# A decoder layer on one core: x added to five row blocks by accumulating transfers, the residual kept in the output's place, and two kinds of endings

## The chip, the cores and the metric

One NeuronCore of a Trainium2 chip runs the whole kernel; the metric is the device time of one execution in microseconds. The engines are TensorE (PE, with its weight loads PEld), VectorE (DVE), ScalarE (ACT), GpSimd (POOL) and SyncE (SP, which only issues DMA transfers here). Each engine works its own instructions in the order in which the program wrote them, and waits on semaphores for the others.

## The reference

One layer of a hybrid decoder, 1024 rows of 1024 columns, float32:

```python
h = rms_norm(h_res, pre_mix_g)            # h_res = 16 meta rows, then x
proj = h @ w_in                           # q1 q2 k1 k2 v u
o = rms_norm(diff_attention(...), subln_g) * 0.8
y = rms_norm(glu(gelu(s5_ssm(u))), ssm_out_g)
mix = concat([o, y]) @ w_out
h_res = h_res + rms_norm(mix, post_mix_g)           # the first residual
h = rms_norm(h_res, pre_ffn_g)
f = (silu(h @ w_gate) * (h @ w_up)) @ w_down
h_res = h_res + rms_norm(f, post_ffn_g)             # the second residual
return h_res[:, 16:]
```

The meta rows are dropped from the output, so both residuals are needed for the 1024 rows of x alone.

## The kernel before, in words

Rows are handled in eight blocks of 128, numbered t_ = 0 to 7. The mixed output of block t_ collects in the SBUF tile `part[t_]` (128 x 1024): matmuls leave `mix` banks in PSUM, and DVE adds them to the tile. Attention ends with the late blocks first; the order in which the blocks are complete is `ORD` = 6, 7, 4, 5, 2, 3, 0, 1.

`chain_t` then makes the first residual of a block: ACT squares `part` with a sum (`jk<-part`), DVE and POOL make the root (`rstd`: a tiny DVE instruction, then a power on POOL), DVE scales the block by the root and the gain (`part<-part,ms,gpm`), and DVE or POOL, whichever the planner thinks is done earlier, adds x, which SP has loaded into a tile `xr` (a ring of three). The sum stands in `xr`. ACT squares it, ACT's queue stores it to the DRAM tensor `h_d` (`act_dma`), a second root is made, and ACT or DVE writes the scaled block back to `part`. `ht_stream` transposes that on PE; from there the FFN's products start.

The FFN is a recursion with seven products in place of eight, in float32 split into a high and a low part (`unit`: a cast on ACT, a difference on DVE or POOL). Weight units stand in slots of SBUF (`slot`), of which `sl_add` opens a number with each pool. The products of gate and up end in PSUM banks `PA` and `PS`; those of the down projection in `dn` banks, which `xacc_stream` adds to accumulators X (`XA`, `XS` in the profile). Between the two, the units of silu(gate) * up go to DRAM (`fu_d`) and come back as `dA` and `dS`.

`out_t` ends a block: SP loads the first residual from `h_d` into `hr`, DVE adds the last banks, ACT squares the two halves with sums (`jkf`), DVE or POOL multiplies each half by the gain `gpf`, DVE and POOL make the root (`ms<-ssf`, then the power), DVE multiplies each half by the root and adds the residual in one instruction (`XA<-XA,ms,rr` and the like), and SP stores the half to the output. Blocks 4 to 7 and 0 to 3 end in pairs, q = t_ % 4 going from 0 to 3; the last pair is blocks 7 and 3.

The order of all instructions is written by a planner when the program is built (`Plan`). Every stream above is a generator that yields the engine and the tiles it needs next; the planner keeps a clock for each engine from its own prices, and always lets the stream go on whose need is met earliest. So a new price or a new step changes the order of what follows. `TUNE` holds small offsets for streams by stretches of the planner's own time.

Of the kernel before, what the change touches and what calls it, by code (L numbers as in the profile page):

```python
# [8 lines left out]
F32 = mybir.dt.float32  # L9
# [29 lines left out]
SCRATCH = 1024  # L39
SEG = 40.0  # L40
# [337 lines left out]
def W(fn):  # L378
    return fn, "pe"
# [13 lines left out]
def build(tc, I, out):  # L393
# [12 lines left out]

    st = ExitStack()
# [72 lines left out]
    h_d = dr.tile([NX, D], F32, name="h_d")  # L480
# [1380 lines left out]
    def chain_stream():  # L1861
        yield W(lambda: "wo" in flag and "kv" in flag)
        om = open_pool(om_es, "om")
        gpm = om.tile([P, D], F32, name="gpm")
        sp.dma_start(out=gpm, in_=I["post_mix_g"][0].partition_broadcast(P))
        S["om"] = om, gpm, om.tile([P, D], BF16, name="jk")
        wp["early"] = {}
        for n, t_ in enumerate(ORD):
            yield W(lambda: n < NXR or ORD[n - NXR] in hdone)
            xr = T_(om, [P, D], F32, "xr", "xr", NXR)  # L1870
            sp.dma_start(out=xr, in_=I["x"][0, t_ * P:(t_ + 1) * P, :])
            xrs[t_] = xr
        yield W(lambda: len(hdone) == T and "raw0" in flag and "hT" in flag)
        om_es.close()
        pt_es.close()
        flag["om"] = True
        plan.fill = None

    def early_stream():
        yield W(lambda: "om" in S and len(xrs) >= XR0)  # L1880
# [13 lines left out]
    XR0 = 2  # L1894
    xrs, odone, hdone = {}, set(), set()

    def chain_t(t_):
        yield W(lambda: t_ in odone and t_ in xrs and wp.get("y", 0) > t_)
        om, gpm, jk = S["om"]
        xr, pt = xrs[t_], part[t_]  # L1900
# [10 lines left out]
        else:  # L1911
# [3 lines left out]
            eng = "pool" if plan.end("pool", 2.0) < plan.end("dve", 2.0) else "dve"  # L1915
            yield G(eng, pt, xr)
            (pool if eng == "pool" else dve).tensor_tensor(xr, pt, xr, ALU.add)
# [3 lines left out]
        act_dma(h_d[t_ * P:(t_ + 1) * P, :], xr)  # L1921
# [12 lines left out]
    def ffn_open():  # L1934
# [13 lines left out]
        sl_add(pa, 6)  # L1948
# [16 lines left out]
    CS = [2, 3, 3, 3]  # L1965
    DORD = ["A11", "S3", "S2", "S1", "A12", "S4", "A22"]
# [433 lines left out]
    def out_t(t_):  # L2400
        q = t_ % 4
        yield W(lambda: "dn" in flag)
        hr = raw_new()
        sp.dma_start(out=hr, in_=h_d[t_ * P:(t_ + 1) * P, :])
# [6 lines left out]
        for d, n in zip(ds, names):  # L2411
# [8 lines left out]
            e = less("dve", "pool")  # L2420
            yield G(e, xs[d])
            engs[e].tensor_tensor(xs[d], xs[d], gpf[:, d * 512:d * 512 + 512], ALU.mult)
# [6 lines left out]
        for d in ds:  # L2429
            cs = slice(d * 512, d * 512 + 512)  # L2430
            yield G("dve", ms, xs[d])
            dve.scalar_tensor_tensor(xs[d], xs[d], ms, hr[:, cs], ALU.mult, ALU.add)
            sp.dma_start(out=out[0, t_ * P:(t_ + 1) * P, cs], in_=xs[d])
        raw_free(hr)
# [53 lines left out]
```

## Time and profile before

| | us |
|---|---|
| median of 3 runs | 1256.05 |
| lowest and highest run | 1255.34, 1260.98 |
| the profiled execution, its own time | 1258.01 |
| its span, first to last instruction | 1256.2 |
| busy in the span: PE / PEld / DVE / ACT / POOL | 1193.3 / 1009.7 / 936.7 / 585.8 / 637.8 |

The span is what the rows below are taken from; times in them count from its start. A busy share over the whole span mixes stages with different limits.

### The profile page before, as it was taken

What the parts mean: (1) busy time and instruction counts of PE and PEld (TensorE: products, weight loads), DVE (VectorE), ACT (ScalarE), POOL (GpSimd) and SP (SyncE); (2) the same over time, 40 slices, a digit from 0 to 9 for tenths busy, and PEclk for the clock granted to TensorE, in tenths of its full rate; (3) what the DMA queues carried; (4) which work ended last, traced back from release to release, by engine and by line L of the source; (5) the groups of instructions that cost most, each with busy time, mean ns of one, the idle gap of its engine ahead of it and who ended that gap; (6) DMA issues with size and microseconds to landing.
All of it is one profiled execution on the core that took longest, in us unless ns stands there. A gap on an engine that the chain in (4) does not pass through costs nothing.

```text
span 1256.2 us, 19391 instructions
## 1 busy us (share of the span) xinstructions
PE 1193.3 (95%) x6808; PEld 1009.7 (80%) x6808; DVE 936.7 (75%) x1678; ACT 585.8 (47%) x1203; POOL 637.8 (51%) x663
## 2 busy tenths in 40 slices
PE   8999989999999999888999999999999989999994
PEld 6999979988888788667878888888888868888873
DVE  5978886664857879898667877668665876466998
ACT  6323323245756556656456456454555544222122
POOL 1015556413423023555666666677676765455735
PEclk9999989999999999989999999999999999999997
DMA  8254434316421013232244434344334479766563
GB/s 245 78 108 102 99 96 98 98 60 188 167 69 51 26 51 118 84 109 85 85 167 163 156 101 167 135 177 153 112 135 161 187 275 413 277 216 227 197 251 134
DMA packets 155490, 182.89 MB, mean 146 GB/s; under 512 B 72017, under 2 KB 122481, under 8 KB 155393
## 3 DMA queue, kind: packets, MB, share of 16 engines
q1 hardware_dynamic: 153056, 177.38, 42.4%
q10 hardware_dynamic: 2336, 4.26, 0.9%
q8 instruction: 54, 0.88, 0.3%
q14 instruction: 44, 0.35, 0.1%
HBM read 117.52 MB, written 61.44 MB: 142 GB/s over the span
## 4 chain that ended last, share of the span: by engine, by line
PE 73%; DVE 10%; POOL 6%; DMA 4%; issue 3%; ACT 2%; SPq 1%; DVEq 0%; POOLq 0%; ACTq 0%
PE PS L246 17%; PE PA L246 12%; PE dn L246 12%; PE pqk L246 6%; PE mix L246 6%; PE pv L246 5%; PE pu L246 3%; PE s L246 3%; DVE XS L246 2%; PE z L246 2%; DVE part L246 1%; DVE XA L246 1%; PE aT L246 1%; PE pm L246 1%; DMA x<-in_x 1%
## 5 line engine op out<-in xcount | busy, mean ns | idle before, releaser
L246 PE MATMUL PS<-BT,uS 128*128 128x512 f32 x792 | 193.8, 399 | 2.9 <-ACT uS L246 1.8
L246 PEld LDWEIGHTS PS<-BT,uS 128*128 128x128 f32 x792 | 149.9, 190 | 40.5 <-ACT uS L246 2.3
L246 PE MATMUL PA<-B,uA 128*128 128x512 f32 x528 | 134.3, 403 | 3.3 <-DVE B L246 3.1
L246 PE MATMUL dn<-dS,dS 128*128 128x512 f32 x528 | 126.3, 399 | 5.3 <-DMA dS<-fu_d 5.3
L246 PEld LDWEIGHTS dn<-dS,dS 128*128 128x128 f32 x528 | 101.0, 192 | 28.9 <-DMA dS<-fu_d 5.7
L246 PEld LDWEIGHTS PA<-B,uA 128*128 128x128 f32 x528 | 100.4, 191 | 28.0 <-DVE B L246 3.4
L246 PE MATMUL dn<-dA,dA 128*128 128x512 f32 x396 | 93.7, 393 | 2.4 <-DVE dA L246 2.4
L246 PEld LDWEIGHTS dn<-dA,dA 128*128 128x128 f32 x396 | 74.2, 188 | 19.8 <-DVE dA L246 2.8
L246 ACT CAST uS<-rr 128x512 fp32r<-128x512 f32 x84 | 50.4, 618 | 53.1 <-DVE rr L246 37.9
L246 PE MATMUL pqk<-wlo,hTh 128*128 128x256 f32 x256 | 73.0, 285 | 1.8 <-DVE wlo L246 1.8
L246 PE MATMUL pqk<-whi,hTh 128*128 128x256 f32 x256 | 74.4, 291 | 0.0
L246 PE MATMUL pqk<-whi,hTl 128*128 128x256 f32 x256 | 72.8, 284 | 0.0
L246 ACT ACTIVATE rr<-rr,gffT 128x256 f32<-128x256 f32 x168 | 72.2, 498 | 0.6 <-DMA rr<-in_w_up 0.6
L246 POOL TENSOR_TENSOR uS<-rr,uS 128x512 fp32r<-128x512 f32 x41 | 60.9, 1497 | 21.1 <-ACT uS L246 18.6
L246 POOL TENSOR_TENSOR uA<-rr,uA 128x512 fp32r<-128x512 f32 x30 | 43.5, 1451 | 53.2 <-ACT uA L246 47.4
L246 PE MATMUL PS<-B,uS 128*128 128x512 f32 x264 | 65.5, 397 | 0.0
L246 PE MATMUL PA<-BT,uA 128*128 128x512 f32 x264 | 65.4, 396 | 0.0
L246 POOL TENSOR_TENSOR ms<-ms,mhalf 128x1 f32<-128x1 f32 (+1 forms) x41 | 25.5, 625 | 70.8 <-DVE ms L246 58.4
L246 DVE TENSOR_TENSOR uA<-rr,uA 128x512 fp32r<-128x512 f32 x30 | 31.7, 1057 | 39.7 <-ACT uA L246 39.2
L246 DVE TENSOR_REDUCE nmx<-s 128x1 f32<-128x528 f32 (+8 forms) x60 | 47.9, 809 | 16.4 <-PE s L246 16.3
L246 PEld LDWEIGHTS PA<-BT,uA 128*128 128x128 f32 x264 | 49.7, 188 | 12.1
L246 PEld LDWEIGHTS PS<-B,uS 128*128 128x128 f32 x264 | 49.7, 188 | 12.1
(467 smaller groups left out, 3326.1 us busy)
## 6 DMA issues: line engine op xcount, KB each, us to landing
fu_d<-fS SPq DMA_DIRECT2D x44, 512.0 KB, 2.8
dS<-fu_d SPq DMA_DIRECT2D x44, 512.0 KB, 5.2
fu_d<-fA SPq DMA_DIRECT2D x33, 512.0 KB, 3.1
dA<-fu_d SPq DMA_DIRECT2D x33, 512.0 KB, 5.1
rr<-in_w_up SPq DMA_DIRECT2D x22, 512.0 KB, 4.4
rr<-in_w_gate SPq DMA_DIRECT2D x20, 512.0 KB, 4.8
rr<-in_w_down SPq DMA_DIRECT2D x10, 512.0 KB, 5.7
raw<-qk_d SPq DMA_DIRECT2D x6, 768.0 KB, 5.7
```

Of the source, the lines that this page charges most:

```text
L246: r = real(*a, **kw)
```

## The change

In the first residual, the first five blocks of `ORD` (`NXA = 5`: 6, 7, 4, 5, 2) no longer load x into `xr`. Their sum is made in `part` itself: POOL's queue issues a transfer from x in DRAM onto the tile that adds what it brings (`add_dma`, `accum_op`). The store of the sum follows directly in the program, on ACT's queue, ahead of the square; for the other three blocks the add and the store stay as they were. All eight blocks are stored to the output tensor's own rows instead of `h_d`, which is gone.

In the endings, only the blocks with q = 3 (`LATE`: 7 and 3) load the residual back, from the output, and end as before, with the multiplications by the gain put on DVE except for one half. The other six blocks multiply by root and gain in one DVE instruction, and POOL's queue issues a transfer for each half that adds it to the output in DRAM.

A pool of weight slots gets seven in place of six, and the early loads of weights wait for the same number of x loads as before, counted anew. The planner's prices for the new transfers are in `add_dma`.

```diff
--- before.py
+++ after.py
@@ -37,6 +37,7 @@
 
 BIAS = {}
 SCRATCH = 1024
+NXA = 5
 SEG = 40.0
 TUNE = {
     0: {'gate_stream': -0.04, 'ssm_u_stream': -0.23, 'proj_stream': 0.39, 'ynorm_stream': 0.0},
@@ -404,6 +405,13 @@
         plan.clk["act"] += 0.5
         plan.sent(out, src, plan.clk["act"])
 
+    def add_dma(out, src):
+
+        plan.flush((plan.tid(out), plan.tid(src)))
+        nc.gpsimd.dma_start(out=out, in_=src, accum_op=ALU.add)
+        plan.clk["pool"] = max(plan.clk["pool"], plan.wrote(src, "pool")) + 1.0
+        plan.sent(out, src, plan.clk["pool"] + 3.5)
+
     st = ExitStack()
     st.enter_context(tc.manual_schedule())
     cp = st.enter_context(tc.tile_pool(name="cp", bufs=1))
@@ -477,7 +485,6 @@
     u_d = dr.tile([L, 512], F32, name="u_d")
     v_d = dr.tile([L, 512], F32, name="v_d")
     qk_d = dr.tile([H, L, 384], F32, name="qk_d")
-    h_d = dr.tile([NX, D], F32, name="h_d")
     y_d = dr.tile([NX, 512], F32, name="y_d")
     fu_d = dr.tile([NF // 2, 7, P, D], F32, name="fu_d")
 
@@ -1865,8 +1872,10 @@
         sp.dma_start(out=gpm, in_=I["post_mix_g"][0].partition_broadcast(P))
         S["om"] = om, gpm, om.tile([P, D], BF16, name="jk")
         wp["early"] = {}
-        for n, t_ in enumerate(ORD):
-            yield W(lambda: n < NXR or ORD[n - NXR] in hdone)
+        for t_ in ORD[:NXA]:
+            xrs[t_] = None
+        for n, t_ in enumerate(ORD[NXA:]):
+            yield W(lambda: n < NXR or ORD[NXA + n - NXR] in hdone)
             xr = T_(om, [P, D], F32, "xr", "xr", NXR)
             sp.dma_start(out=xr, in_=I["x"][0, t_ * P:(t_ + 1) * P, :])
             xrs[t_] = xr
@@ -1877,7 +1886,7 @@
         plan.fill = None
 
     def early_stream():
-        yield W(lambda: "om" in S and len(xrs) >= XR0)
+        yield W(lambda: "om" in S and len(xrs) >= NXA + XR0)
         om = S["om"][0]
         raw0 = [om.tile([P, 4, 256], F32, name=f"raw0{d}") for d in range(2)]
         for d in range(2):
@@ -1891,13 +1900,14 @@
                 r = wp["early"][m, A_] = T_(om, [P, 4, P], F32, "early", "early", NER)
                 sp.dma_start(out=r, in_=wv[w][:, 4 * d:4 * d + 4, 256 * j:256 * j + P])
 
-    XR0 = 2
+    XR0 = min(2, T - NXA)
     xrs, odone, hdone = {}, set(), set()
 
     def chain_t(t_):
         yield W(lambda: t_ in odone and t_ in xrs and wp.get("y", 0) > t_)
         om, gpm, jk = S["om"]
-        xr, pt = xrs[t_], part[t_]
+        pt = part[t_]
+        xr = xrs[t_] or pt
         ssq = col("ssq")
         yield G("act", pt)
         act.activation(jk, pt, AF.Square, accum_out=ssq)
@@ -1912,13 +1922,19 @@
             r = yield from rstd(ssq, 1.0 / D)
             yield G("dve", r)
             dve.scalar_tensor_tensor(pt, pt, r, gpm, ALU.mult, ALU.mult)
-            eng = "pool" if plan.end("pool", 2.0) < plan.end("dve", 2.0) else "dve"
-            yield G(eng, pt, xr)
-            (pool if eng == "pool" else dve).tensor_tensor(xr, pt, xr, ALU.add)
+            if xr is pt:
+                yield G("pool", pt)
+                add_dma(pt, I["x"][0, t_ * P:(t_ + 1) * P, :])
+                act_dma(out[0, t_ * P:(t_ + 1) * P, :], xr)
+            else:
+                eng = "pool" if plan.end("pool", 2.0) < plan.end("dve", 2.0) else "dve"
+                yield G(eng, pt, xr)
+                (pool if eng == "pool" else dve).tensor_tensor(xr, pt, xr, ALU.add)
         ssq = col("ssq")
         yield G("act", xr)
         act.activation(jk, xr, AF.Square, accum_out=ssq)
-        act_dma(h_d[t_ * P:(t_ + 1) * P, :], xr)
+        if xr is not pt:
+            act_dma(out[0, t_ * P:(t_ + 1) * P, :], xr)
         r = yield from rstd(ssq, 1.0 / D)
         if plan.clk["act"] + 0.4 < plan.clk["dve"]:
             yield G("act", r)
@@ -1945,7 +1961,7 @@
         yield W(lambda: "om" in flag)
         rsv.clear()
         pa = open_pool(pa_es, "pa")
-        sl_add(pa, 6)
+        sl_add(pa, 7)
         wp["pa"] = pa
         raw_add([(pa, f"rr{j}") for j in range(4)])
         yield W(lambda: "A" in flag)
@@ -1963,6 +1979,7 @@
 
     NU, NRQ, MD, KEEP = 9, 3, 8, 2
     CS = [2, 3, 3, 3]
+    LATE = (3,)
     DORD = ["A11", "S3", "S2", "S1", "A12", "S4", "A22"]
 
     QUARTERS = {"S2": (("S2", "A11"), ("S3", "S2")), "S1": (("S2", "S1"), ("S1", "S3")),
@@ -2399,9 +2416,11 @@
 
     def out_t(t_):
         q = t_ % 4
-        yield W(lambda: "dn" in flag)
-        hr = raw_new()
-        sp.dma_start(out=hr, in_=h_d[t_ * P:(t_ + 1) * P, :])
+        late = q in LATE
+        if late:
+            yield W(lambda: "dn" in flag)
+            hr = raw_new()
+            sp.dma_start(out=hr, in_=out[0, t_ * P:(t_ + 1) * P, :])
         yield W(lambda: q in comb_done)
         pb, gpf, X = wp["pb"], wp["gpf"], wp["acc"]
         ssq = T_(pb, [P, 2], F32, "ssf", "ssf", 8)
@@ -2417,9 +2436,10 @@
                 free(t)
             yield G("act", xs[d])
             act.activation(wp["jkf"], xs[d], AF.Square, accum_out=ssq[:, d:d + 1])
-            e = less("dve", "pool")
-            yield G(e, xs[d])
-            engs[e].tensor_tensor(xs[d], xs[d], gpf[:, d * 512:d * 512 + 512], ALU.mult)
+            if late:
+                e = "dve" if n != "S1" else less("dve", "pool")
+                yield G(e, xs[d])
+                engs[e].tensor_tensor(xs[d], xs[d], gpf[:, d * 512:d * 512 + 512], ALU.mult)
         ms = T_(sm, [P, 2], F32, "ms", "ms", 16)[:, :1]
         yield G("dve", ssq)
         dve.tensor_tensor(ms, ssq[:, 0:1], ssq[:, 1:2], ALU.add)
@@ -2429,9 +2449,15 @@
         for d in ds:
             cs = slice(d * 512, d * 512 + 512)
             yield G("dve", ms, xs[d])
-            dve.scalar_tensor_tensor(xs[d], xs[d], ms, hr[:, cs], ALU.mult, ALU.add)
-            sp.dma_start(out=out[0, t_ * P:(t_ + 1) * P, cs], in_=xs[d])
-        raw_free(hr)
+            if late:
+                dve.scalar_tensor_tensor(xs[d], xs[d], ms, hr[:, cs], ALU.mult, ALU.add)
+                sp.dma_start(out=out[0, t_ * P:(t_ + 1) * P, cs], in_=xs[d])
+                continue
+            dve.scalar_tensor_tensor(xs[d], xs[d], ms, gpf[:, cs], ALU.mult, ALU.mult)
+            yield G("pool", xs[d])
+            add_dma(out[0, t_ * P:(t_ + 1) * P, cs], xs[d])
+        if late:
+            raw_free(hr)
 
     plan.run([
         start(), psum_stream(),
```

## Rows read from the trace of the kernel before

**Rows 1.** The table of windows, of core 0. Columns: the window and its length, then for PE, PEld, DVE, ACT and POOL the busy time (and the number of instructions), then TensorE's granted clock as a share of full speed, the busy share of the DMA engines, and GB/s.

```profile
490.00:555.00 65.00, 56.59 (x351) 45.60 (x351) 58.08 (x114) 43.75 (x101) 36.18 (x53) 0.97 0.26 94
...
645.00:1015.00 370.00, 369.51 (x1571) 296.97 (x1572) 269.36 (x306) 196.59 (x395) 255.24 (x173) 1.00 0.42 151
1015.00:1040.00 25.00, 19.68 (x75) 15.66 (x74) 17.54 (x19) 12.94 (x25) 17.39 (x12) 0.86 0.86 310
```

**Rows 2.** The timeline of 502 to 508.4 us, all engines, around the add of block 6, the first in the order. Columns of every timeline: start, duration, engine, line, operation, what it writes <- what it reads, shapes, count, and in brackets how long the engine stood before it and what ended that.

```profile
502.20 1.27 DVE L246 SCALAR_TENSOR_TENSOR part<-part,ms,gpm 128x1024 f32<-128x1024 f32 x1
...
503.56 2.37 POOL L246 TENSOR_TENSOR xr<-part,xr 128x1024 f32<-128x1024 f32 x1 [1.94 <-DVE rl L246]
503.59 2.36 DVE L246 SCALAR_TENSOR_TENSOR co<-ls,rl,lamv 128x1 f32<-128x1 f32 x1
...
505.97 0.33 ACTq L403 DMA_DIRECT2D h_d<-xr  x1
...
507.15 0.38 ACT L246 ACTIVATE E<-s,nmx 128x144 f32<-128x144 f32 x1
...
508.29 0.15 DVE L246 RECIPROCAL rl<-ls 128x1 f32<-128x1 f32 x1
```

**Rows 3.** The timeline of 516 to 523 us, around the add of block 7.

```profile
516.54 1.28 DVE L246 SCALAR_TENSOR_TENSOR part<-part,ms,gpm 128x1024 f32<-128x1024 f32 x1
...
517.92 2.37 DVE L246 SCALAR_TENSOR_TENSOR co<-ls,rl,lamv 128x1 f32<-128x1 f32 x1
...
521.36 0.24 ACT L246 CAST AT<-aT 128x128 fp32r<-128x128 f32 x1
```

**Rows 4.** The timeline of 525 to 543 us, around the adds of blocks 4, 5 and 2, in this order.

```profile
525.50 1.28 DVE L246 SCALAR_TENSOR_TENSOR part<-part,ms,gpm 128x1024 f32<-128x1024 f32 x1
...
527.68 0.28 ACT L246 CAST AT<-aT 128x128 fp32r<-128x128 f32 x1
...
528.20 1.22 DVE L246 TENSOR_TENSOR xr<-part,xr 128x1024 f32<-128x1024 f32 x1
...
530.14 1.28 DVE L246 SCALAR_TENSOR_TENSOR part<-part,ms,gpm 128x1024 f32<-128x1024 f32 x1
...
531.98 2.39 POOL L246 TENSOR_TENSOR xr<-part,xr 128x1024 f32<-128x1024 f32 x1
...
535.59 1.06 ACT L246 ACTIVATE jk<-part 128x1024 bf16<-128x1024 f32 x1
...
539.07 1.27 DVE L246 SCALAR_TENSOR_TENSOR part<-part,ms,gpm 128x1024 f32<-128x1024 f32 x1
...
542.09 0.39 ACT L246 CAST oT<-ov 128x256 fp32r<-128x256 f32 x1
```

**Rows 5.** DMA issues by what they write and read: the issuing queue, operation, count, KB of each, median us from issue to landing.

```profile
xr<-in_x SPq DMA_DIRECT2D x8, 512.0 KB, 3.7
h_d<-xr ACTq DMA_DIRECT2D x8, 512.0 KB, 2.6
rq<-in_w_down SPq DMA_DIRECT2D x7, 512.0 KB, 7.2
...
out<-XA SPq DMA_DIRECT2D x8, 256.0 KB, 2.1
```

**Rows 6.** DVE's groups of instructions from 1213 us to the end, shapes kept apart. Columns: line, engine, operation, written <- read, shapes, count | busy us in all, mean ns of one | idle us before them, and what ended it.

```profile
L246 DVE TENSOR_TENSOR ms<-ssf 128x1 f32<-128x1 f32 x8 | 5.5, 692 | 0.0
L246 DVE SCALAR_TENSOR_TENSOR XS<-XS,ms,rr 128x512 f32<-128x512 f32 x4 | 4.0, 1007 | 0.1
L246 DVE SCALAR_TENSOR_TENSOR XA<-XA,ms,rr 128x512 f32<-128x512 f32 x4 | 3.0, 748 | 0.1
L246 DVE TENSOR_TENSOR XS<-XS,gpf 128x512 f32<-128x512 f32 x4 | 2.8, 689 | 2.0 <-ACT jkf L246 2.0
L246 DVE TENSOR_TENSOR dA<-rq,dA 128x512 fp32r<-128x512 f32 x1 | 1.6, 1590 | 0.0
...
L246 DVE TENSOR_TENSOR XA<-XA,gpf 128x512 f32<-128x512 f32 x2 | 1.4, 686 | 0.3 <-ACT jkf L246 0.3
L246 DVE TENSOR_SCALAR ms<-ms 128x1 f32<-128x1 f32 x8 | 1.2, 154 | 0.3
```

**Rows 7.** POOL's groups in the same stretch, same columns.

```profile
L246 POOL TENSOR_TENSOR XA<-XA,gpf 128x512 f32<-128x512 f32 x6 | 9.7, 1613 | 5.4 <-ACT jkf L246 5.4
L246 POOL TENSOR_TENSOR XS<-XS,gpf 128x512 f32<-128x512 f32 x4 | 5.4, 1361 | 9.5 <-ACT jkf L246 9.5
L246 POOL TENSOR_TENSOR ms<-ms,mhalf 128x1 f32<-128x1 f32 x8 | 4.7, 597 | 4.1 <-DVE ms L246 4.1
```

**Rows 8.** The timeline of the last stretch: the last matmuls of PE, the last bank add of DVE and the last store of SP's queue.

```profile
1236.67 2.23 PE L246 MATMUL dn<-dA,dA 128*128 128x512 f32 x9
...
1246.79 0.68 DVE L246 TENSOR_TENSOR XA<-dn,XA 128x512 f32<-128x512 f32 x1
...
1253.09 0.33 SPq L191 DMA_DIRECT2D out<-XA  x1
```

**Rows 9.** Timelines of PE and of SP's queue: PE's two longest stops after 600 us (each in the brackets of the row behind it), and the store on SP's queue ahead of the loads of the second.

```profile
644.14 0.74 PE L246 MATMUL PS<-BT,uS 128*128 128x512 f32 x2 [1.83 <-ACT uS L246]
...
1019.88 0.32 SPq L191 DMA_DIRECT2D fu_d<-fA  x1
...
1031.83 13.25 PE L246 MATMUL dn<-dS,dS 128*128 128x512 f32 x45 [5.32 <-DMA dS<-fu_d]
```

## The prediction

> **What bounds the kernel now.** I read the table of windows by stage first [rows 1], since the average hides that the stages have different limits. From 645 to 1015 us TensorE (PE) is busy 369.51 of 370 us: whatever the change does to other engines in there is worth nothing unless it makes PE wait. Two stretches are different, and they are the two that the change edits. From 490 to 555 us (the end of attention, and the chains that make the residual) PE stands still for 8.4 us and DVE is busy 58.08 of 65 us. From 1211 us to the end DVE is the pace: PE's last matmul ends at 1236.67 + 2.23 = 1238.9 us, DVE still has bank adds to do at 1246.79 us, and the last store is issued at 1253.09 us [rows 8]. So I read these two stretches instruction by instruction [rows 2 to 4, 6, 7], and then the one long stop of PE between them [rows 9].
>
> In [rows 2] the reader should see three things around block 6, the first of the five. DVE ends the scaling of the block at 503.47 us. POOL then adds x for 2.37 us, and a DVE instruction on one column takes 2.36 us beside it: DVE is held while POOL's add runs. And DVE gets going on new ACT results at 508.29 us, after exponentials that start on ACT at 507.15 us. Block 7 repeats it [rows 3]. Blocks 4 and 2 add on DVE (1.22 us for block 4), block 5 on POOL (2.39 us) [rows 4].
>
> **The first part: x added by transfers.** Five adds go: three POOL instructions, two of which hold DVE for some 2.2 us, and two DVE instructions of 1.2 us. Five of the eight loads of x on SP's queue go too; their landing (3.7 us median, [rows 5]) was covered by the ring of three buffers, so they gave nothing back. What comes: on POOL's queue, for each block, one issue of a 512 KB accumulating transfer that waits for DVE's scaling; and on ACT's queue the store of the block, now written directly behind the transfer's issue instead of behind the square. That store must wait until the sum has landed, and a wait on ACT holds all that is written behind it there: exponentials, the casts of AT and oT, the squares. The planner doesn't know: it books 0.5 us for the store on ACT and goes on. So the price of a block is not the add but how long ACT's queue stands: call it L, from the end of DVE's scaling to the landing.
>
> How long may ACT stand before it costs more than the add did? From the end of the scaling to the first ACT instruction that DVE or the mix needs next, plus the DVE add where one is removed:
> block 6: 507.15 - 503.47 = 3.7 us [rows 2]; block 7: 521.36 - 517.82 = 3.5 us [rows 3]; block 4: 527.68 - 526.78 + 1.2 = 2.1 us; block 5: 535.59 - 531.42 = 4.2 us; block 2: 542.09 - 540.34 + 1.2 = 3.0 us [rows 4]. Together 16.5 us. The stage is tied from ACT to DVE to PE and back, so I let what is beyond that go through one to one: cost = 5L - 16.5.
>
> No accumulating transfer and no issue on POOL is in this trace. L is bounded below by the store of the same block from ACT, 2.6 us to landing plus its 0.33 us issue, 2.9 us in all (cost -2.0), and above by the load of 512 KB into a busy stretch, 7.2 us (cost +19.5) [rows 2, 5]. I take the nearest row, the load of the same rows of x into the same kind of tile, 3.7 us, and 0.3 us more for POOL's issue: L = 4.0 us, cost +3.5 us. The Trainium skill (DMA: Bandwidth & Descriptors, "Anatomy of one DMA — SWDGE (gpsimd) path") fits a transfer issued from GpSimd as 2.0 us and its bytes at 436 GB/s; an estimate by it is 3.2 us for 512 KB, which would make this stage -0.5 us and the forecast 4 us lower. No run here shows it yet.
>
> In this part the scaling back into the block's own tile must also wait for its store; it lies behind square and root, some 3 us after landing, which about covers the 2.6 us store. The last three blocks, whose latency PE waits for, keep their add.
>
> **The second part: the endings.** For six of the eight row blocks the gain multiplies in the instruction that already applied the root (same size, so no price), and the residual is added by POOL's transfer into the output. Removed from DVE between 1213 us and the end [rows 6, 7]: POOL now does ten multiplications by the gain, and DVE's eight tiny sums (ms<-ssf) take 5.5 us where eight neighbours of that size take 1.2 us, so 4.3 us of holds; four scalings average 1007 against 748 ns, 1.0 us more; one split took 1.59 us where a product of that size takes 0.69, 0.9 us more. Of DVE's own six multiplications (2.8 + 1.4 us) three stay for the last two blocks: 2.1 us saved, and about half of the 2.3 us in which DVE waited for the square before them, 1.2 us. That is 9.5 us; one POOL multiplication may stay, with a hold of 1.1 us, so 8.4 to 9.5 us. The other bound is PE: its last matmul ends at 1238.9 us, and the same add, square, root, scaling and store behind the last bank take 6.3 us, from the bank add at 1246.79 to the last store's issue at 1253.09 us, and 2.1 us of landing [rows 5, 8]: 1247.3 against the span's 1256.2 us, 8.9 us. I take these 8.9 us. The stores of the last two blocks stay on SP; the six loads of the residual that go were hidden anyway: no idle time of DVE there ends with a load [rows 6].
>
> **Between them.** The planner writes a new order for everything after the first chain, with one more weight slot. I book -1 us: half of the 1.83 us stop at 644 us [rows 9], which an earlier unit could fill. PE-bound from there to 1015 us, a new order is otherwise free.
>
> **The sum.** +3.5 - 8.9 - 1.0 = -6.4 us. The profiled execution took 1258.0 us (span 1256.2 us and 1.8 us around it), 2 us above the median of the runs; on it that is 1251.6, on the median of 1256.05 us it is **1249.6 us**.
>
> **The rivals.**
> *ACT's queue stands longer (slower).* Everything hangs on L: beyond 5.3 us the first part eats the 9.9 us of the rest. For it: an accumulating transfer also reads what it adds to, POOL must issue it while DVE is nearly always busy, and the planner's own price from issue to landing is 1.0 + 3.5 + 1.2 + 1.5 + 0.9 = 8.1 us. Against it: the DMA engines are a quarter busy in this stretch [rows 1], and the same x rows land in 3.7 us. At L = 7.2 us: 1256.05 + 19.5 - 9.9 = 1265.6 us. The Trainium skill (SBUF — State Buffer, "SBUF: two separate sides") says that GpSimd can't write the descriptors of its transfers while DVE holds the port that the two share; by it L grows here. The trace agrees on the lock with the roles turned: DVE held for 2.36 us by a 2.37 us POOL add [rows 2].
> *POOL becomes the pace of the endings.* Nine multiplications go (about 13.6 us of POOL, [rows 7]), twelve issues come; over 13.6 / 12 = 1.13 us each, roots (0.6 us) queue behind them. An issue lies between ACT's 0.33 us and POOL's add of a whole block, 2.39 us [rows 2, 4]. At 1.8 us POOL has 8 us more than before and the second part is worth about 1 us: 1256.05 + 3.5 - 1 - 1 = 1257.5 us.
> *The stop at 1026 us goes.* PE waits 5.32 us for a load that sat behind a store on SP's queue until 1019.88 us [rows 9], and runs that stretch at a granted clock of 0.86, some 3 us more [rows 1]. Another order or one more slot can remove it: 1249.6 - 8 = 1241.6 us. Against it: only one slot more, and the same queue. A new order may as well lengthen it.
>
> **Chances and range.** The forecast's case 0.40 (within 1244 to 1255), ACT's queue 0.30, POOL's pace 0.14, the stop gone 0.12, else 0.04. About 0.5% (6.3 us) is what a measurement of this kernel can tell from no change. Faster by more: 0.30 of the first and the 0.12 of the stop, 0.42. Within: 0.10 of the first, 0.05 of ACT's case near L = 5.3 us, 0.11 of POOL's and 0.03 else, 0.29. Slower: the rest, 0.29. The range goes from 1239 (the stop gone and L some 0.5 us under 4.0) to 1266 us (L = 7.2 us).
>
> **What will show it.** On ACT, the gap behind each of the first five stores from its queue, which is L less some 0.5 us; DVE's one-column instructions at 0.2 us beside them; the first matmul of the FFN some 3 us later. In the endings, eight ms<-ssf near 0.15 us, POOL issues of about 1 us, PE's end unchanged and the last store some 7 us behind it. Wrong would be: L over 5 us, that matmul late by more than 6 us, roots that wait behind issues, or a longer stop at 1026 us.

## The result, and the profile after

The changed kernel takes 1270.94 us (median of 4 runs, 1270.22 to 1272.87) against 1257.18 us of the kernel before on the same chip (one run more than in the table of before): 1.0116 times its time, with a 95% interval of 1.0093 to 1.014. It is slower by 13.8 us by the medians; the forecast was 6.4 us faster. The profiled execution of it took 1272.87 us, its span 1271.1 us.

Where the time went is seen by five marks in the trace of each kernel (us from the start of the span; the end of the last row of its kind, and for the scaling of block 6 and the last store the start):

| | scaling of block 6 | last transpose | last PA product | last dn product | last store |
|---|---|---|---|---|---|
| before | 502.20 | 591.0 | 1015.0 | 1238.9 | 1253.1 |
| after | 505.06 | 611.2 | 1030.4 | 1258.4 | 1267.9 |
| difference | 2.9 | 20.2 | 15.4 | 19.5 | 14.8 |

The first 2.9 us are not the change's: they arise before 45 us, and the first column varies between 501.6 and 507.3 us over the kernels below. So the stage of the chains loses 17 us, the long products give back 5, the products of the down projection lose 4, and the ending gives back 5.

**The stage.** The table of windows of the kernel after, with the columns of [rows 1]:

```profile
490.00:555.00 65.00, 47.97 (x291) 40.98 (x290) 41.80 (x95) 31.78 (x83) 23.32 (x44) 0.89 0.31 74
645.00:1015.00 370.00, 370.00 (x1581) 297.43 (x1580) 279.34 (x319) 201.89 (x409) 247.91 (x168) 1.00 0.43 152
```

In the first window every engine does less than in [rows 1]: PE 47.97 us where it did 56.59 (1.3 and 5.1 us of these are filling products, `warm`, which the planner puts where PE would stand and whose results nobody uses), DVE 41.80 where it did 58.08. Nothing is overloaded; all wait, and TensorE's granted clock is 0.89 where it was 0.97. For what, the timeline of 505 to 514 us tells, the piece that answers to [rows 2]:

```profile
505.06 1.28 DVE L247 SCALAR_TENSOR_TENSOR part<-part,ms,gpm 128x1024 f32<-128x1024 f32 x1
...
506.44 0.22 DVE L247 SCALAR_TENSOR_TENSOR co<-ls,rl,lamv 128x1 f32<-128x1 f32 x1
506.67 1.10 POOL L411 DMA_DIRECT2D part<-in_x  x1 [2.21 <-DVE co L247]
...
512.67 0.35 ACTq L404 DMA_DIRECT2D out<-part  x1
513.07 0.38 ACT L247 ACTIVATE E<-s,nmx 128x144 f32<-128x144 f32 x1 [6.39 <-DMA part<-in_x]
...
513.93 0.16 DVE L247 RECIPROCAL rl<-ls 128x1 f32<-128x1 f32 x1 [4.84 <-ACT E L247]
```

DVE's one-column instruction is down from 2.36 to 0.22 us, as forecast. But behind it the bracket of ACT's exponential says 6.39 us of standing, ended by the landing of the adding transfer, and DVE's bracket 4.84 us, ended by that exponential. Three of the other four blocks show the same on ACT; block 4's scaling ends while ACT already stands for block 7, so its wait falls into the same standing (timeline of 530 to 566 us):

```profile
534.88 0.35 ACTq L404 DMA_DIRECT2D out<-part  x1
535.28 0.47 ACT L247 ACTIVATE ov<-pv,g 128x256 f32<-128x256 f32 x1 [6.32 <-DMA part<-in_x]
538.16 0.34 ACTq L404 DMA_DIRECT2D out<-part  x1
...
549.96 0.27 ACT L247 CAST AT<-aT 128x128 fp32r<-128x128 f32 x1 [6.71 <-DMA part<-in_x]
...
564.67 1.06 ACT L247 ACTIVATE jk<-part 128x1024 bf16<-128x1024 f32 x1 [8.23 <-DMA part<-in_x]
```

From the end of the scaling to the store behind it the five blocks take 6.3, 5.8, 5.9, 5.8 and 7.1 us: 6.2 us on average, where the forecast had L = 4.0. The transfer is most of it: POOL's issue starts 0.3 us behind the scaling, and from the start of the issue (which itself takes 0.9 us) to the landing it is 5.8 us on average, 5.6 in the median. The DMA issues (columns of [rows 5]) give the medians; the endings' transfers are below:

```profile
part<-in_x POOLq DMA_DIRECT2D x5, 512.0 KB, 5.6
out<-part ACTq DMA_DIRECT2D x5, 512.0 KB, 2.7
...
out<-XA POOLq DMA_DIRECT2D x6, 256.0 KB, 4.7
out<-XS POOLq DMA_DIRECT2D x6, 256.0 KB, 5.0
```

PE loses by it twice. The windows of 510 to 520 and of 530 to 540 us, around the first two holds:

```profile
510.00:515.00 5.00, 0.41 (x2) 0.19 (x1) 1.00 (x4) 1.93 (x6) 0.63 (x3) 1.00 0.66 181
515.00:520.00 5.00, 3.96 (x19) 3.77 (x19) 4.12 (x12) 3.75 (x15) 1.14 (x4) 0.52 0.00 2
530.00:535.00 5.00, 0.89 (x4) 0.38 (x2) 1.38 (x2) 0.00 (x0) 1.82 (x3) 1.00 0.73 119
535.00:540.00 5.00, 3.60 (x15) 3.31 (x16) 1.56 (x4) 2.64 (x6) 0.99 (x2) 0.57 0.95 279
```

PE stands for most of a hold (0.41 and 0.89 of 5 us busy), and when it has work again its granted clock is 0.52 and 0.57, close to the lower level of 1.2 GHz (0.50). The planner has also put fewer filling products into this stage, 20 where there were 40; hold and filling were not parted as causes of the lower clock.

**The products.** The stop at 644 us [rows 9] is gone. The one behind `fu_d` is 4.34 us where it was 5.32, and two come that nobody forecast (PE's timeline of 1030 to 1230 us):

```profile
1046.31 12.75 PE L247 MATMUL dn<-dS,dS 128*128 128x512 f32 x45 [4.34 <-DMA dS<-fu_d]
...
1214.19 10.13 PE L247 MATMUL dn<-dS,dS 128*128 128x512 f32 x36 [3.97 <-DVE dS L247]
1226.46 6.89 PE L247 MATMUL dn<-dS,dS 128*128 128x512 f32 x29 [2.15 <-DVE dS L247]
```

**The endings.** DVE's and POOL's groups from 1214 us to the end, with the columns of [rows 6]:

```profile
L247 DVE SCALAR_TENSOR_TENSOR XA<-XA,ms,gpf 128x512 f32<-128x512 f32 x6 | 4.5, 747 | 2.3 <-POOL ms L247 2.3
L247 DVE SCALAR_TENSOR_TENSOR XS<-XS,ms,gpf 128x512 f32<-128x512 f32 x6 | 4.4, 747 | 1.9 <-POOL ms L247 1.9
L247 DVE TENSOR_TENSOR ms<-ssf 128x1 f32<-128x1 f32 x8 | 1.3, 156 | 1.9 <-ACT jkf L247 1.9
L247 POOL TENSOR_TENSOR ms<-ms,mhalf 128x1 f32<-128x1 f32 x8 | 6.0, 788 | 5.2 <-DVE ms L247 5.0
L411 POOL DMA_DIRECT2D out<-XS x6 | 5.6, 926 | 3.1 <-DVE XS L247 2.8 <-issue 0.2
```

The holds are gone: the sums `ms<-ssf` take 156 ns where they took 692. In their place DVE waits 4.2 us for POOL's powers in these two groups, where the same two groups had 0.2 us of idle time before [rows 6]; POOL's issues are 0.93 us each. One of the roots, from the timelines of DVE and POOL: its sum is ready at 1248.68 us, two issues go ahead of the power on POOL, and DVE can scale at 1251.40 us, 2.7 us later.

```profile
1248.53 0.15 DVE L247 TENSOR_SCALAR ms<-ms 128x1 f32<-128x1 f32 x1
1248.84 0.90 POOL L411 DMA_DIRECT2D out<-XA  x1 [1.20 <-DVE ms L247]
1249.93 0.86 POOL L411 DMA_DIRECT2D out<-XS  x1 [0.20 <-issue]
1250.50 0.87 POOL L247 TENSOR_TENSOR ms<-ms,mhalf 128x1 f32<-128x1 f32 x1
1251.40 0.75 DVE L247 SCALAR_TENSOR_TENSOR XS<-XS,ms,gpf 128x512 f32<-128x512 f32 x1 [0.66 <-POOL ms L247]
```

From PE's last product to the last store it is 9.5 us, where it was 14.2.

### The profile page after: what moved, and what is told of

Same layout as the page of the kernel before. It is cut to its first block, busy times and chain, and to the rows that moved or that the text cites. A ratio compares the mean times of both kernels' runs of the same rounds, so it can differ in the third digit from the quotient of the medians.

```text
span 1271.1 us, 19429 instructions
## 1 busy us (share of the span) xinstructions
PE 1200.8 (94%) x6861; PEld 1017.7 (80%) x6861; DVE 928.5 (73%) x1686; ACT 583.2 (46%) x1202; POOL 616.3 (48%) x656
## 4 chain that ended last, share of the span: by engine, by line
PE 43%; DVE 18%; POOL 15%; issue 10%; ACT 7%; DMA 5%; SPq 1%; POOLq 0%; ACTq 0%; DVEq 0%
PE dn L247 11%; PE pv L247 6%; PE mix L247 6%; PE pqk L247 5%; POOL rr L247 3%; PE pu L247 3%; PE s L247 3%; POOL fS L247 2%; POOL uA L247 2%; DMA part<-in_x 2%; DVE XS L247 2%; ACT rr L247 2%; DVE XA L247 2%; DVE rr L247 1%; DVE part L247 1%
## 5 line engine op out<-in xcount | busy, mean ns | idle before, releaser
L247 POOL TENSOR_TENSOR uA<-rr,uA 128x512 fp32r<-128x512 f32 x32 | 47.2, 1475 | 50.6 <-ACT uA L247 46.0
L247 POOL TENSOR_TENSOR uS<-rr,uS 128x512 fp32r<-128x512 f32 x38 | 55.4, 1467 | 26.1 <-ACT uS L247 26.1
L247 POOL TENSOR_TENSOR rr<-rr,rr 128x512 f32<-128x512 f32 x37 | 53.7, 1452 | 16.6 <-DVE rr L247 7.7
L247 PEld LDWEIGHTS PA<-BT,uA 128*128 128x128 f32 x264 | 49.7, 188 | 12.2
```

What stands on the lines that cost most here:

```text
L247: r = real(*a, **kw)
```

## The experiments

The kernels were timed beside the kernel before, whose median in these comparisons lay between 1256.1 and 1256.8 us; I reckon with 1256.6. Only the kernel of experiment 4 ran a single time. "Six slots" is `sl_add(pa, 6)`, as before. Each edit is to the changed kernel. Experiments 5 and 6 carry the edit of experiment 1 too, which does nothing where no block is added by a transfer.

**1. The store behind the square.** Nothing is taken out; ACT's queue no longer meets the wait first.

```diff
                 add_dma(pt, I["x"][0, t_ * P:(t_ + 1) * P, :])
-                act_dma(out[0, t_ * P:(t_ + 1) * P, :], xr)
 ...
         act.activation(jk, xr, AF.Square, accum_out=ssq)
-        if xr is not pt:
-            act_dma(out[0, t_ * P:(t_ + 1) * P, :], xr)
+        act_dma(out[0, t_ * P:(t_ + 1) * P, :], xr)
```

> The changed kernel with one edit: for the five blocks the store of the sum stands behind the square again, so that ACT's queue meets it when the planner thinks the sum has landed. If ACT's queue held by the store is the cause, the waits of over 6 us on ACT for the landing of x shrink below 3 us each, the last transposes end some 12 us earlier than the 611 us of the changed kernel, and the time is 1256 to 1261 us. If the late sum itself is the cause (the block is ready 5 us later, whoever waits), the gain is under 4 us: 1267 us or more. If the new order of the planner is the cause, nothing in particular is expected, and the transposes need not move.

Measured: 1255.76 us, ratio 1.0005 (0.9992 to 1.0017). The last transpose ends at 590.3 us. The time is just under the expected 1256 to 1261 us, and the transposes end 21 us earlier where 12 were expected. The landing still takes 5.6 us, but of the five blocks only two leave a wait on ACT, one of them above the 3 us that were expected (timeline of ACT, then the window of 490 to 555 us):

```profile
509.21 1.06 ACT L247 ACTIVATE jk<-part 128x1024 bf16<-128x1024 f32 x1 [0.50 <-DMA part<-in_x]
...
550.54 1.06 ACT L247 ACTIVATE jk<-part 128x1024 bf16<-128x1024 f32 x1 [5.52 <-DMA part<-in_x]
```

```profile
490.00:555.00 65.00, 61.38 (x397) 50.80 (x398) 53.40 (x112) 41.24 (x98) 32.49 (x55) 1.00 0.37 86
```

Between the scaling of block 6 and the square of its sum, the first row, ACT now works on the exponentials and casts that stood behind the store; PE is busy for 61.38 us where it was 47.97 (6.1 and 1.3 us of these are filling products), at a clock of 1.00 where it was 0.89. One line's place is worth 15.2 us, and the transfers are still there. The edit also makes the planner write another order for what follows, so by itself it doesn't part the hold from the order; experiment 4 keeps the order.

**2. The endings alone**, `NXA = 0`.

> The changed kernel without its first part (NXA = 0: x is loaded and added by DVE or POOL in all eight blocks); the endings, the residual in the output's place and the seventh slot stay. If the first part is the cause of the loss, by the queue or by the late sum, the transposes end near 591 us as before and the time is that of the kernel before less what the endings give, some 5 us from PE's end to the last store and 0 to 4 us back for PE's new stops near its end: 1250 to 1256 us. If the planner's new order is the cause, it stays above 1262 us.

Measured: 1258.32 us, ratio 1.0017 (1.0002 to 1.0031), slower than the expected 1250 to 1256 us and far from the rival's 1262. So the first part costs 12.6 us in the changed kernel (1270.94 less 1258.32). The last store is 8.8 us behind PE's last product (14.2 before), but PE ends later: its stops of 4.02 us at 1200 and 2.15 us at 1212 us are here too. So they don't come from the first part.

**3. The first part alone**, endings of before, six slots.

```diff
-        sl_add(pa, 7)
+        sl_add(pa, 6)
-    LATE = (3,)
+    LATE = (0, 1, 2, 3)
-                e = "dve" if n != "S1" else less("dve", "pool")
+                e = less("dve", "pool")
```

> The changed kernel with the endings of before for all blocks and six slots; the first part alone, with the residual in the output's place. If the first part costs what the traces show in its stage (17 us later at the last transposes, of which some 4 us come back by the stop at 644 us), the time is 1268 to 1275 us. If the loss comes from the endings or from the seventh slot, it is within 4 us of the kernel before.

Measured: 1264.31 us, ratio 1.0083 (1.0051 to 1.0115): 7.7 us slower by the medians, below the expected 1268 us and above the rival's 4 us. There are four runs, three between 1263.0 and 1265.4 us and one of 1271.95 us, and that one is the profiled execution, so its trace tells where this kernel waits and not what its median is made of. In it ACT stands for 6.19, 6.04, 6.76 and 8.64 us as in the changed kernel; the two new stops of PE are gone with the slot and the endings, and the stop behind `fu_d` is 1.31 us. Why the median loses less than the 12.6 us that the first part costs in the changed kernel stays open; by the interval the loss is 6.4 to 14.5 us.

**4. The same transfers without the adding**: the five blocks' mixed output is overwritten by x and so left out of the result; the waits stay, and every engine works the same instructions in the same order as in the changed kernel.

```diff
-        nc.gpsimd.dma_start(out=out, in_=src, accum_op=ALU.add)
+        if out.space == DRAM:
+            nc.gpsimd.dma_start(out=out, in_=src, accum_op=ALU.add)
+        else:
+            nc.gpsimd.dma_start(out=out, in_=src)
```

> The changed kernel with the five transfers of x from POOL's queue made plain: they overwrite the block instead of adding to it, so the scaled mixed output of five blocks is left out of the result; all instructions and their order stay. It splits the 5.6 us from issue to landing. If the adding in the transfer is what makes it long, the plain one lands in 3 to 4 us like the loads of the same rows on SP's queue, ACT's waits shrink by 2 us each, and the time falls by about 8 us to some 1263 us. If the issue from POOL is what makes it long, it still takes over 5 us and the time stays within 3 us of 1271 us.

Measured, in a single run: 1260.78 us, 10 us less than with the adding, and the last transpose ends 9.5 us earlier from the same start of the stage. The landing is 4.1 us where the adding one's is 5.6 (medians), and an issue on POOL, which is a part of it, takes 0.58 us in place of 0.93 (timeline of POOL, then the DMA issues):

```profile
529.16 0.57 POOL L414 DMA_DIRECT2D part<-in_x  x1 [1.62 <-DVE part L247]
539.13 0.58 POOL L414 DMA_DIRECT2D part<-in_x  x1 [1.62 <-DVE rs L247]
```

```profile
part<-in_x POOLq DMA_DIRECT2D x5, 512.0 KB, 4.1
```

From the end of the scaling to the store it is 4.4 us on average where it was 6.2: adding costs some 1.8 us per 512 KB here, the longer issue included. Five blocks by 1.8 us are 9 us of the 10 measured: with the order kept, what the store holds ACT's queue for passes on nearly one to one in the sum over the five. This shows the hold as a cause without a change of order. It is one run, and the runs of one kernel lie some 3 us to either side of their median.

**5. The seventh slot alone**: `NXA = 0` and the endings of before, seven slots.

> The changed kernel with no block added by transfers and all eight endings as before: of the change only the seventh weight slot (and the residual stored in the output's place) is left. Theory (the slot makes PE's stops): with the seventh slot the planner may start a weight unit earlier, and it writes one split dS of that unit on DVE behind 22 accumulator adds; PE then stops about 4.0 us near 1200 us and about 2.1 us near 1212 us for DVE dS, as in the changed kernel and in the run of the endings alone, where the kernel before has one stop of 2.4 us. PE's last product some 3.5 us later than before, and the time 2 to 5 us above the kernel before. Rival (the new endings make the stops, their work stands ahead of the split on DVE): without the endings the only stop in that stretch is near 2.4 us and the time is that of the kernel before, within 1.5 us.

Measured: 1259.00 us, ratio 1.0017 (1.0001 to 1.0033), 2.4 us above 1256.6 and barely clear of the noise. PE's stops are there without the new endings (the second is 1.50 us), and DVE and ACT show how they arise (timelines of ACT, DVE and PE around 1195 us):

```profile
1194.25 0.62 ACT L247 CAST dS<-rq 128x512 fp32r<-128x512 f32 x1
...
1199.15 0.68 DVE L247 TENSOR_TENSOR XS<-dn,XS 128x512 f32<-128x512 f32 x1
1199.75 1.28 DVE L247 TENSOR_TENSOR dS<-rq,dS 128x512 fp32r<-128x512 f32 x2
...
1200.48 10.77 PE L247 MATMUL dn<-dS,dS 128*128 128x512 f32 x36 [4.01 <-DVE dS L247]
```

ACT's cast is done at 1194.9 us; DVE's difference to it starts 4.9 us later, since DVE works through accumulator adds that the program has put ahead of it, without a pause. PE stands until it is done. PE's last product ends at 1244.7 us, 5.8 us later than before, but the last store comes only 1.6 us later: the old endings, in which DVE ends long after PE, seem to cover most of it.

**6. The endings with six slots**, `NXA = 0`.

> The changed kernel with no block added by transfers and six weight slots in place of seven: the endings alone, without the slot. Theory (the endings do shorten the tail, the slot took it back): PE's stops behind DVE in the last products fall from 6.2 to about 2.4 us, the last store stays 9 to 10 us behind PE's last product (14.2 us before), and the time is 3 to 5 us under the kernel before, about 1253. Rival (the endings give nothing because POOL's issues hold up the roots): the time stays that of the endings with seven slots, 1258, and that of the kernel before, within 1.5 us. The forecast's own term, 8.9 us, would give 1248.

Measured: 1251.96 us, ratio 0.9965 (0.995 to 0.998). PE's stops behind DVE are gone (0.8 and 0.9 us behind ACT and POOL are left), the last store is 10.3 us behind PE's last product. The endings by themselves are worth 4.6 us, and the slot costs them 6.4. They stay 4.3 us short of the forecast's 8.9, and DVE's waits from 1205 us on are where this may lie (columns: who waited for what, us in all, times, longest); before, it waited 0.3 us for POOL's powers there:

```profile
DVE XS L247 <- POOL ms L247: 2.7, 3, 1.4
DVE ms L247 <- ACT jkf L247: 2.0, 3, 1.0
DVE XA L247 <- POOL ms L247: 1.5, 3, 0.7
```

**7. Both parts, store behind the square, six slots.**

> The changed kernel with the store of the five blocks behind the square and with six slots: both parts of the change, without ACT's held queue and without the slot. Theory: the run with the store behind the square stood at 1255.8 with PE's two new stops; without them some 3.5 us less, 1251 to 1253, and if the adds by transfers are worth 2 us of their own (the difference of the two runs before, 1258.3 and 1255.8), 1250. Rival (the stops are not the slot's): 1255 to 1257.

Measured: 1250.25 us, ratio 0.9947 (0.9928 to 0.9966), 6.4 us faster than before: two edits turn the loss into a gain of the forecast's size. Of it 4.6 us are there without any transfer into `part` (experiment 6); the 1.7 us between the two are not clear of the noise.

**8. The first part with the store behind the square, alone**: experiment 3 with the edit of experiment 1.

> The changed kernel with the store of the five blocks behind the square, all eight endings as before and six slots: the adds by transfers alone, without ACT's held queue. Theory (the whole loss of the first part is the held queue): the run with the first part alone stood at 1264.3; without the held queue some 15 us of its stage go, less what the store behind the square still waits: 1251 to 1256, at or just under the kernel before, the last transposes near 590 us. Rival (the adding transfers cost by themselves, by their latency from scaling to landing of 6.3 us): the last transposes near 600 us or later and the time 1261 or more.

Measured: 1255.69 us, ratio 0.9995 (0.9979 to 1.0011); the last transpose at 591.2 us. The rival falls: a latency of some 6 us from scaling to sum costs nothing here while ACT has other work to do. Nor is the first part worth anything alone that can be told from the noise.

**9. Two blocks with the held queue**, `NXA = 2`, six slots.

> The changed kernel (store of the sum ahead of the square on ACT's queue) with two blocks, 6 and 7, in place of five, and six slots. The endings with six slots and no block added by transfers stood at 1252.0. Theory (each block passes on what its held queue exceeds its own break-even, one to one): with 6.3 us from the end of the scaling to the landing the two blocks cost 6.3 - 3.7 = 2.6 and 6.3 - 3.5 = 2.8 us, 5.4 in all, so about 1257.4. Rival (the stage has slack that takes the first blocks, the loss comes only as they pile up): within 1.5 us of 1252.0.

Measured: 1254.53 us, ratio 0.9991 (0.9979 to 1.0004), 2.6 us above experiment 6: between the two expectations. In the stage it is worse than either: the last transpose ends 12.2 us later than in experiment 6, of which 1.9 us are there at the first scaling, so two holds of 6.1 and 6.2 us lose 10.3 us and no break-even is seen. Behind each hold the granted clock is at the lower level (0.50 from 515 to 520 and from 535 to 540 us, 1.00 there in experiment 6), and this part of the loss the prediction did not have; its share was not separated. Later the stops at 643 us vanish and the one behind `fu_d` falls from 4.0 to 2.1 us in two pieces. The price of one block, as the prediction worked it out, is therefore not confirmed; only the sum over five was near.

**10. Four blocks in the endings in place of six**, `LATE = (2, 3)`, the rest as 7.

> The run with the store behind the square and six slots (1250.3), with the blocks of q = 2 (6 and 2) ended as before too: four accumulating blocks in the endings in place of six. Four POOL issues of 0.9 us go, four multiplications by the gain of 0.7 us come, at least three of them on DVE. Theory (POOL's issues pace the endings, the roots queue behind them): DVE's waits for POOL's powers fall by half, 1 to 2 us faster, 1248.5 to 1249.5. Rival (DVE is the pace): 2 us slower, 1252 to 1253. If both hold in part, within 1 us of 1250.3.

Measured: 1253.93 us, ratio 0.9989 (0.9974 to 1.0004), 3.7 us above experiment 7 by the medians, though the two profiled spans differ by 0.6 us only. DVE's waits for POOL's powers fall from 4.8 to 2.4 us, as the first theory says, and the time does not follow. DVE has the multiplications in their place; that this is why was not tested. The time is above both expectations.

**11. All eight blocks added by transfers**, `NXA = 8`, the rest as 7.

> The run with the store behind the square and six slots (1250.3), with all eight blocks added by transfers. The adding transfer takes 6.3 us from the end of the scaling to the landing where an add on DVE took 1.2 and on POOL 2.4 us, and the last blocks' latency stands in front of the FFN's first products. Theory (latency decides there): the last block alone delays the last transposes by 6.3 - 2.4 = 3.9 us or more: 1254 or slower, with the last transposes at 594 us or later. Rival (other work hides it): within 1.5 us of 1250.3.

Measured: 1244.04 us, ratio 0.9911 (0.9891 to 0.9931). Both expectations were too slow: this beats both kernels. The last transpose is at 588.4 us, 1.7 us earlier than in 7. The windows of 560 to 570, 570 to 580, 595 to 645 and 1015 to 1040 us, of experiment 7 and then of this one:

```profile
560.00:570.00 10.00, 4.85 (x26) 3.53 (x24) 6.68 (x11) 5.22 (x9) 7.82 (x7) 0.80 0.20 82
570.00:580.00 10.00, 8.49 (x83) 7.66 (x83) 8.10 (x10) 4.91 (x10) 7.95 (x6) 0.69 0.00 0
595.00:645.00 50.00, 48.32 (x204) 38.26 (x203) 32.50 (x40) 27.78 (x57) 32.35 (x23) 1.00 0.37 132
1015.00:1040.00 25.00, 20.27 (x82) 16.22 (x82) 18.34 (x19) 14.48 (x27) 19.00 (x13) 0.93 0.91 339
```

```profile
560.00:570.00 10.00, 9.69 (x123) 8.72 (x122) 7.34 (x12) 6.49 (x13) 6.15 (x6) 1.00 0.95 261
570.00:580.00 10.00, 9.13 (x131) 8.59 (x128) 7.20 (x12) 5.55 (x10) 6.89 (x7) 1.00 0.01 2
595.00:645.00 50.00, 50.00 (x215) 40.21 (x214) 35.86 (x44) 28.40 (x58) 32.36 (x22) 1.00 0.38 130
1015.00:1040.00 25.00, 23.43 (x103) 18.86 (x102) 17.51 (x19) 13.41 (x25) 15.99 (x12) 1.00 1.03 416
```

In 7, PE is busy for 4.85 of 10 us and its granted clock falls to 0.69 of full speed in the next window, a mixture of the two levels (0.60 and 0.50 from 565 to 575 us, 0.50 being 1.2 GHz); with eight blocks PE is busy for 9.69 and 9.13 us, since 96 of its 123 and 103 of its 131 instructions are the planner's filling products (`warm`), and the clock stays at 1.00. The stops between 595 and 645 us are gone, and the stop behind `fu_d` falls from 4.73 to 1.57 us. So the latency of the last blocks, which I took for the danger, did not show as a loss. The order is a new one, and which of these pieces brings how much of the gain was not separated.

**12. All eight blocks alone**, store behind the square, endings of before, six slots.

> All eight blocks added by transfers, the store behind the square, all eight endings as before, six slots: the first part alone, in its larger form. The same with five blocks stood at 1255.7 and the kernel before at 1256.6; with the new endings five blocks stood at 1250.3 and eight at 1244.0. Theory (the last three adds are worth their 6 us in front of the products: the last transposes near 588 us, no stop of PE between 590 and 645 us, the half-clock stretch near 570 us gone), so the gain is there without the endings too: 1249 to 1251. Rival (the gain came only together with the endings' order): 1255 to 1257.

Measured: 1247.92 us, ratio 0.993 (0.9911 to 0.9948), 7.8 us below experiment 8 and a little faster than expected. The gain of the last three blocks is there without the endings, and again PE is busy for 50.00 of the 50 us from 595 to 645 us with the clock at 1.00 from 555 us on. The new endings add 3.9 us to it.

## Why the prediction was wrong

**What bounds the kernel** held in part. The stage around 490 to 555 us and the ending are two places where the change acted, and of the 17 us that the stage lost the long products gave back 5. But a third place lost 4 us, the last products of the down projection, and the forecast had no term for it.

**Two steps failed, of about the same size.** The forecast was 1249.6 us, 21.3 us too fast. Experiment 2, the change without its first part, splits this. The first part, beside the rest, costs 12.6 us where +3.5 was forecast. The endings with the seventh slot cost 1.7 us where -8.9 and -1.0 were forecast. These are 9.1 and 11.6 us; 0.6 us are the kernel before, 1256.6 in place of 1256.05. So the right L alone would not have saved the forecast: with 6.2 us its sum gives 1256.05 + 14.5 - 9.9 = 1260.7 us, still 10 us short.

**The first part, L.** The mechanism was named, as the term and as the first rival: ACT's queue stands from the scaling to the landing, and more than the adds gave back. The size was off. L was put at 4.0 us by the nearest row, a load of the same bytes into the same kind of tile from another queue; measured are 6.2. That row is near for a plain transfer from POOL (4.1 us to landing, experiment 4), but the adding one takes 5.6 us. The two bounds, 2.9 and 7.2 us, held it; the choice between them by likeness was the failing step. "Does the transfer add" had no row, and I let it cost nothing (the 0.3 us more were for POOL's issue), although the first rival's argument, that it reads what it adds to, stood in the same text. The estimate by the Trainium skill (DMA: Bandwidth & Descriptors, "Anatomy of one DMA — SWDGE (gpsimd) path"), 3.2 us, is below both measured values, 4.1 us plain and 5.6 us adding. The same rival's other argument, that POOL must issue while DVE is busy, was not tested by itself.

With 6.2 us the prediction's own formula gives 5 x 6.2 - 16.5 = +14.5 us in place of +3.5. It is a net price, so what answers to it are the 12.6 us of the changed kernel (experiment 2), or the 7.7 us of the first part alone (experiment 3), not the 15.2 us between the two places of the store. That it comes near 12.6 is in part luck. Experiment 9 lost 10.3 us in the stage with two blocks, where the formula gives 2 x 6.2 - 7.2 = 5.2, and 2.6 us at the end. Block 4's hold falls into block 7's standing. The break-even of block 5 was read past a cast of AT that starts 0.1 us behind its scaling (531.42 us), and in the changed kernel it is a cast of AT that stands behind this block's store (549.96 us):

```profile
531.51 0.26 ACT L246 CAST AT<-aT 128x128 fp32r<-128x128 f32 x1
```

By the prediction's own rule, then, block 5 has 0.1 us to spare and not 4.2. And the lower clock behind each hold, 0.52 and 0.57, was put at nothing in this stage. The last step, "one to one", holds where the order is kept (experiment 4); over changes of order it depends on the rest of the kernel: the hold is worth 15.2 us in the changed kernel and 8.6 with the old endings and six slots (experiments 3 and 8).

**The endings.** The forecast took 8.9 us, by the bound of PE's end; measured alone with six slots are 4.6. The bound was 1.0 us too wide as worked out: it ends at the last store's landing, but the span before ends 1.0 us behind that landing (1253.09 + 2.1 = 1255.2 against 1256.2 us), so 7.9 us was the most by it. That the holds would go (ms<-ssf near 0.15 us) and that POOL's issues would be about 1 us was right. Wrong was to take POOL's issues as harmless below 1.13 us: that weighed POOL's sum of work, and the sum is indeed smaller. But each root is one small POOL instruction that DVE waits for, and it stands behind whatever issue is ahead of it in the program: 4.2 us of waits for powers came where 4.3 us of holds went. This is the second rival's place with a lesser price. That these waits make up the missing gain is argued, and experiment 10, which halved them, was not faster.

**Between them.** The stop at 644 us went, as booked. The seventh slot was taken as free, "PE-bound from there to 1015 us, a new order is otherwise free". It cost 2.4 us alone and 5.5 to 6.4 us with the new endings, by a split that the new order puts behind DVE's accumulator adds. The prediction looked at where PE already stood and asked which stops could go; a stop that does not exist yet has no row, and the rivals had the slot only as a gain, in the third. That it costs more with the new endings fits experiment 5, where the old endings cover most of PE's later end.

**The third rival**, the stop at 1026 us goes, did not happen in the change (4.34 us). In experiments 3, 9, 11 and 12 it shrank to 0.3 to 1.8 us a piece; what sets it stays open.

**The sum.** By experiments: endings -4.6, slot +5.5 (experiments 1 and 7), five adds by transfers -1.7 (6 and 7), the held queue +15.2: +14.4 us. These are steps along one row of kernels from before to after, so they add up to the whole whatever the cause, and the fit proves nothing. Timed alone the parts are endings -4.6, slot +2.4 and first part +7.7: +5.5 us, 9 us less than the 14.3 of all together. The parts are not independent, and a sum of terms that were each taken alone could not have found it. The forecast's -6.4 us is what experiment 7 gave, by other terms than forecast; that is a coincidence.

## What to carry to other kernels

A DMA start on a compute engine's queue is an instruction in order: when its source is still being written, everything behind it on that engine stands, so put it behind work that is ready, or behind the engine's own use of the same data. Price a transfer that adds by itself and not by the plain one of the same size, and ask of a small instruction on a shared queue (a root on POOL) what stands ahead of it, not how full the queue is. Time a small side edit, such as one more buffer, by itself and beside what it comes with: here it hid the gain of the endings in full. And where a hold leaves PE idle, look at the granted clock behind it.

## What the runs showed of the hardware

- An accumulating transfer of 512 KB from DRAM into SBUF landed 5.6 us after the start of its issue on POOL's queue, the plain one 4.1 us (medians of five; experiment 4, same order); the issue took POOL 0.93 against 0.58 us. Accumulating 256 KB into DRAM took 4.7 to 5.0 us, where SP's plain store of 256 KB took 2.1 before [rows 5] and 2.6 in the changed kernel.
- A store on ACT's queue that waited for an adding transfer held ACT's later instructions: 6.4, 6.3, 6.7 and 8.2 us of standing in the changed kernel.
- An add of 128x1024 on POOL held DVE's one-column instruction for 2.36 us [rows 2]. Issues on POOL did not: in the changed kernel the sum `ms<-ssf` at 1241.57 us took 0.15 us beside an issue that ran from 1241.35 to 1242.25 us.
- Behind a stretch in which PE stood for most of the time the granted clock fell to the lower level: 0.50 from 570 to 575 us in experiment 7, behind 2.04 of 5 us busy; 0.52 from 515 to 520 us in the changed kernel, behind 0.41 of 5 us. With filling products in that place it stayed at 1.00 (experiments 11 and 12).
